# Spreading the mixer's scale rows later, and the rotated key as a task of its own

## The chip, the cores and the metric

The kernel runs on one core of a Trainium2 chip. The metric is the device time of one execution in microseconds (us), as the median over runs. The product stays on TensorE (PE), with weight loads (PEld) beside it; VectorE (DVE) and ScalarE (ACT) prepare operands and empty the accumulators; SyncE (SP) issues the weight transfers.

## What is computed

Two layers of an encoder over 256 tokens of width 2048, all in float32. Each layer is a mixer and a feed-forward block, both on a normalised input and added back. The mixer is cut here to the parts that the change touches:

```python
h = _rms(x, g_mix[l])
proj = h @ w_in
(ml_q, ml_k, ml_v, ml_o, ml_gates, r_q, r_k, r_v, r_g, c_q, c_kv, k_rope) = split(proj)
q = (_rms(c_q, g_q_norm) @ w_q_up)          # 8 heads of 128 + 64, the 64 rotated
kv = (_rms(c_kv, g_kv_norm) @ w_kv_up)      # 8 heads: 128 of key, 128 of value
k_r = _apply_rope(k_rope[:, :, None, :], cos, sin)   # one rotated key, shared by the heads
# mLSTM: gates -> log sigmoid -> cumulative sums; conv of ml_q, ml_k; 4 heads in two directions
# retention of 4 heads; softmax attention of 8 heads; then @ w_out and the feed-forward block
```

## The kernel before

Every product is made of three: each float32 weight is split into a high half `whi` (ACT, L308) and a low half `wlo` (DVE, L309, the raw weight less `whi`), and so are the activations; PE multiplies high by high, high by low and low by high (L410). Weights come as chunks of 512 KB through `Stream` (L230 to L317): four raw buffers, and four buffers each of `whi` and `wlo`. `get(i)` asks for the halves of chunks up to `i + 2`. So a chunk's halves are written into the buffers that PE freed four chunks earlier, and PE has three chunks in hand.

The activations enter as `xT`, the transposed input, not yet normalised. The factor of a token, `rs` (one over the root mean square), is a per-partition scalar where tokens are on partitions; ACT applies it when it empties an accumulator (`ev_cq` L623, `ev_ckv` L649, `ev_rqk` L942). Where tokens lie along the row, it has to be spread over all partitions: `token_scale` (L534) computes `rs` on DVE, has PE transpose it twice into the bank `rsb` (L542) and copies it to SBUF (L543). In a mixer the first reader of that tile is `ev_qk` (L820), after the product for `ml_q`.

Side work is written as generators, `Task`s (L416). After each four to twelve products the program calls `pump` (L453), which advances a clock `now` by the product's nominal time and steps up to two tasks that are free and due: a task is free once the tasks it depends on are done (or have made so many steps), and due once the delay that it last yielded has passed on that clock. `finish` (L441) runs a task to its end on the spot. All this happens while the program is built: what comes out is one fixed order of instructions per engine, and each engine runs its own order strictly.

The weights of a layer's mixer are taken in the order of `weight_plan`. In layer 0: chunks 0 to 8 are `c_q`, 9 to 14 `c_kv` with the rotated part of the key and the gates, 15 to 22 the retention's `r_qk`, 23 and 24 the keys from the latent part (`kn`), 25 and 26 the values (`v`), 27 to 30 the queries (`qn`), 31 and 32 the queries' rotated part (`qr`), and from 33 on `ml_q`, `ml_k`. The tasks around the change are:

- `rope_tables` (L555), once: cosines and sines for the rotation.
- `cq_task` (L626) and `ckv_task` (L654): normalise the latent parts, transpose them (banks `cqt`, `ckvt`) and split them into `chi`, `clo`. `ckv_task` goes on to rotate the key (`rope` into `kr`, ten instructions on DVE, L670 to L672), has PE transpose it twice (`krt`, L676) and splits it into `krh` and `krl`.
- `gate_task` (L742): eight small transposes on PE (`gi`, `gf`), then a chain of small operations that goes between DVE and ACT: exponential and logarithm on ACT, sums, two groups of four scans (L778, L785), maxima and end weights (L791 to L801) on DVE; a row table to HBM (L804), another exponential, and ten small transposes (`gcol`).
- `qr_task` (L681) rotates the queries; `mla_head` needs it and the rotated key.

The product of chunk 23 on reads `chi`, so the program finishes `ckv_task` before it (L1030).

Of the kernel before, what the change touches and what calls it, by code (L numbers as in the profile page):

```python
# [42 lines left out]
G_MIX, G_FFN, G_ML, G_RET, G_Q, G_KV, W_CONV, B_GATE, PAR_W = 0, 16, 32, 36, 40, 44, 46, 70, 86  # L43
# [277 lines left out]
def encoder_kernel(ctx: ExitStack, tc: tile.TileContext, xin, posin, w, par, const, gfin, out, dump=None):  # L321
# [53 lines left out]
    def bank(name):  # L375
        return pside.tile([P, 512], F32, name=name, tag="s")
# [5 lines left out]
    def rsqrt(dst, src, n, scale):  # L382

        nt = sp.tile([P, 3, n], F32, name="nt", tag=f"nt{n}", bufs=2 if n == 2 else 1)
        v, y, a = nt[:, 0, :], nt[:, 1, :], nt[:, 2, :]
        iv = a.bitcast(I32)
        V.tensor_scalar(v, src, scale, EPS, op0=ALU.mult, op1=ALU.add)
        V.tensor_scalar(iv, v.bitcast(I32), 1, None, op0=ALU.arith_shift_right)
        V.tensor_scalar(y.bitcast(I32), iv, -1.0, float(0x5f3759df), op0=ALU.mult, op1=ALU.add)
        for it in range(3):  # L390
            yield 1.0
            V.tensor_tensor(a, y, y, op=ALU.mult)
            V.scalar_tensor_tensor(a, a, -0.5, v, op0=ALU.mult, op1=ALU.mult)
            V.scalar_tensor_tensor(dst if it == 2 else y, a, 1.5, y, op0=ALU.add, op1=ALU.mult)

    def split(*items):

        for hi, lo, src, *g in items:
            A.activation(hi, src, AF.Copy, **({"scale": g[0]} if g else {}))  # L399
        for hi, lo, src, *g in items:  # L400
            if g:
                V.scalar_tensor_tensor(lo, src, g[0], hi.bitcast(F32), op0=ALU.mult, op1=ALU.subtract)
            else:
                V.tensor_tensor(lo, src, hi.bitcast(F32), op=ALU.subtract)

    def tr(dst, src, n=P):
        T.transpose(dst, src, ident[:n, :n])
# [8 lines left out]
    class Task:  # L416
# [24 lines left out]
        def finish(self, n=1 << 30):  # L441
            for d in self.after:
                d, m = d if isinstance(d, tuple) else (d, 1 << 30)
                d.finish(m)
            while not self.done and self.n < n:
                self.step()

    def add(gen, after=(), delay=0.0):
        t = Task(gen, list(after), delay)
        side.append(t)  # L450
        return t
# [33 lines left out]
    def nat(chunks, lh, ll, evac):  # L485
        ps = [pm.tile([P, 512], F32, name="pm", tag="m") for _ in range(2)]
        nat_steps(chunks, ps, lh, ll, 0, True, True)
        evac(ps)
# [16 lines left out]
    xt_task = {}  # L505
# [12 lines left out]
    def make_xT(b, g0, l, wait):  # L518

        xT = views[1 if g0 == G_FFN else 0]  # L520
        for pr in range(2):
            ps = bank("xt")
            for j in range(2):
                k = 4 * b + 2 * pr + j
                for t in range(2):
                    tr(ps[:, j * S + t * P:j * S + (t + 1) * P], x[t][:, k * P:(k + 1) * P])
            k = 4 * b + 2 * pr
            split(*[(xT[:, k + j, 0, :], xT[:, k + j, 1, :], ps[:, j * S:(j + 1) * S],
                     prm[:, l, g0 + k + j:g0 + k + j + 1]) for j in range(2)])
            yield 0.8 if pr == 0 else wait  # L530
        for t in range(2):
            sumsq(x[t][:, b * 512:(b + 1) * 512], ss[:, t, b:b + 1], 512)

    def token_scale():  # L534
        tot = sp.tile([P, 2], F32, name="tot", tag="tot")
        V.tensor_reduce(tot, ss, axis=AX.X, op=ALU.add)
        yield from rsqrt(rs, tot, 2, 1.0 / D)
        yield 1.0
        rsb = sp.tile([P, 2, P], F32, name="rsb", tag="rsb", bufs=1)
        ps = bank("rsb")  # L540
        for t in range(2):
            tr(ps[:, t * P:(t + 1) * P], rs[:, t:t + 1].broadcast_to([P, P]))  # L542
        V.tensor_copy(hflat(rsb), ps[:, :S])  # L543
        scale_rows.append(rsb)

    def new_xT(b, g0, l, wait=0.8):

        xt_task[b] = add(make_xT(b, g0, l, wait), [(xt_task[b - 1], 2)] if b else [])
        if b == 3:
            xt_last[:] = [add(token_scale(), xt_task.values(), 1.2)]  # L550

    xt_last = []
    scale_rows = []
# [55 lines left out]
    def hflat(tl):  # L609
        return tl.rearrange("p a b -> p (a b)")  # L610

    def layer(l):
        g = prm[:, l, :]
        L = {}
# [39 lines left out]
        def ckv_task():  # L654
            ckv = L["ckv"]
            r = sp.tile([P, 2], F32, name="rckv", tag="rckv", bufs=1)
            yield from rsqrt(r, L["sq"][:, 1, :], 2, 1.0 / 256)
            for t in range(2):
                V.tensor_scalar(ckv[:, t, :256], ckv[:, t, :256], r[:, t:t + 1], None, op0=ALU.mult)
            yield 4.0  # L660
            ps = bank("ckvt")
            for k in range(2):
                for t in range(2):
                    tr(ps[:, k * S + t * P:k * S + (t + 1) * P], ckv[:, t, k * P:(k + 1) * P])
            split(*[(L["chi"][:, 4 + k, :], L["clo"][:, 4 + k, :], ps[:, k * S:(k + 1) * S],
                     g[:, G_KV + k:G_KV + k + 1]) for k in range(2)])
            yield 1.0
            kr = ap.tile([P, 2, P], F32, name="kr", tag="kr")
            krh = L["krh"] = ap.tile([P, S], F32R, name="krh", tag="krh")
            for t in range(2):  # L670
                rope(kr[:, t, :64], ckv[:, t, 256:320], t, 1)
                V.tensor_copy(kr[:, t, 64:], kr[:, t, :64])  # L672
            yield 3.0
            ps = bank("krt")
            for t in range(2):
                tr(ps[:, t * P:(t + 1) * P], kr[:, t, :])  # L676
            A.activation(krh, ps[:, :S], AF.Copy)
            V.tensor_tensor(krl[0:64, :], ps[0:64, :S], krh[0:64, :].bitcast(F32), op=ALU.subtract)


        def qr_task():  # L681
            qr = L["qr"]
            qd = ap.tile([P, 2, 8, 2, 64], F32, name="qd", tag="hlo", bufs=2)
            for t in range(2):
                rope(qd[:, t, :, 0, :], qr[:, t, :], t, 8)
                yield 2.4
                A.activation(qd[:, t, :, 1, :], qd[:, t, :, 0, :], AF.Copy)
                yield 1.2

            qrT = L["qrT"] = ap.tile([P, 8, S], F32R, name="qrT", tag="hhi", bufs=2)  # L690
            for pr in range(4):
                ps = bank("qrt")
                for j in range(2):
                    for t in range(2):
                        tr(ps[:, j * S + t * P:j * S + (t + 1) * P],
                           qd[:, t, 2 * pr + j, :, :].rearrange("p i c -> p (i c)"))
                o = hflat(qrT[:, 2 * pr:2 * pr + 2, :])
                A.activation(o, ps, AF.Copy)
                V.tensor_tensor(o[64:128, :], ps[64:128, :], o[64:128, :].bitcast(F32), op=ALU.subtract)
                yield 1.2  # L700
# [114 lines left out]


        def ev_qk(i, pr, ps):
            if "mt" not in L:
                L["mt"] = ap.tile([P, 2, 4, S], F32, name="mt", tag="hlo", bufs=2)
            V.tensor_tensor(L["mt"][:, i, 2 * pr:2 * pr + 2, :], ps.rearrange("p (a b) -> p a b", a=2),  # L820
                            hflat(scale_rows[-1]).unsqueeze(1).broadcast_to([P, 2, S]), op=ALU.mult)
# [202 lines left out]
        nat(take(), xh, xl, ev_cq)  # L1024
        cqt = add(cq_task(), delay=3.0)
        nat(take(), xh, xl, ev_ckv)
        ckt = add(ckv_task(), [(cqt, 1)] + tables, 2.0)
        gat = add(gate_task(), [(ckt, 4)], 1.0)
        nat(take(), xh, xl, ev_rqk)
        finish(ckt)  # L1030
        L["qT"] = ap.tile([P, 8, S], F32, name="qT", tag="big1")
        L["kT"] = ap.tile([P, 8, S], F32, name="kT", tag="big2")
        L["v"] = ap.tile([P, 2, 1024], F32, name="v", tag="big3")
# [19 lines left out]
                A.activation(L["qr"][:, t, :], ps[t], AF.Copy)  # L1053

        nat(take(), chi(0), clo(0), ev_qr)
        qrt = add(qr_task(), [ckt], 2.0)
        heads = []
        for h in range(8):
            dep = [qrt, ckt] if h == 0 else [(heads[-1], 2)] + heads[-2:-1]
            heads.append(add(mla_head(h), dep, 1.2))  # L1060
        rqt = add(rqk_task(), heads[:1], 1.0)
        cv = []
# [14 lines left out]
        for h in range(4):  # L1077
            dep = [cv[1], gat, heads[-1]] if h == 0 else [(mlh[-1], 3)] + [(t, 7) for t in mlh[-2:-1]]
# [32 lines left out]
        for b in range(2):  # L1111
            nat_steps(take(), pss[b], yh, yl, 0, False, True)
            ev_x(b)(pss[b])
            new_xT(b, G_FFN, l)
# [233 lines left out]
    tables = [add(rope_tables(), [xt_task[3]])]  # L1348
    for l in range(DEPTH):
        layer(l)  # L1350
# [29 lines left out]
```

## Time and profile before

| | us |
|---|---|
| median of 3 runs | 2136.35 (2136.01 to 2136.39) |
| the profiled execution, its own time | 2135.27 |
| its span, first to last instruction | 2133.5 |
| PE busy | 2111.1 (99%) |
| DVE busy | 1607.4 (75%) |
| ACT busy | 1218.1 (57%) |
| PE in the chain that ended last | 94% of the span |

The profiled execution stands 1.1 us under the median. The granted clock of TensorE is 0.997 of full speed on the mean. The busy time of PE counts each product until its modelled end, and products overlap in the pipeline, so distances between starts tell more than busy time.

### The profile page before, as it was taken

To read this page: it belongs to the slowest core of one execution; us is meant where nothing else is said; L and a number is where in the kernel's file an instruction comes from. 1 tells how busy PE (TensorE), PEld (TensorE's weight loads), DVE (VectorE), ACT (ScalarE), POOL (GpSimd) and SP (SyncE) were. 2 spreads that over 40 slices of the span, in tenths; PEclk is the share of its full clock that TensorE was granted. 3 is DMA by queue.
4 is the path that set the end of the run, shared out by engine and by line. 5 is a ranking of instruction groups with operands and counts; after the bars stand their busy time and mean duration, and the time that the engine had idled before them with its cause. 6 is when DMAs were issued, how large, how long until landed. Compare 5 with 4: busy or idle time off the path is not lost.

```text
span 2133.5 us, 29557 instructions
## 1 busy us (share of the span) xinstructions
PE 2111.1 (99%) x11120; PEld 1811.4 (85%) x11120; DVE 1607.4 (75%) x2371; ACT 1218.1 (57%) x1802; POOL 4.4 (0%) x9
## 2 busy tenths in 40 slices
PE   8999999999999999999999999999999999999998
PEld 6898888888888888888888988888888888888887
DVE  5667675788878888887666675758888888788875
ACT  6645655556555555565556456546555556565554
POOL 0000000000000000000000000000000000000000
PEclk9999999999999999999999999999999999999999
DMA  6544555647456566565555354557556575665654
GB/s 211 172 155 133 174 168 189 206 163 240 160 209 208 175 210 204 169 237 164 182 181 171 131 172 139 178 188 224 170 206 200 170 236 161 213 211 175 208 187 158
DMA packets 110527, 394.95 MB, mean 185 GB/s; under 512 B 12328, under 2 KB 13224, under 8 KB 110256
## 3 DMA queue, kind: packets, MB, share of 16 engines
q1 hardware_dynamic: 109072, 389.90, 55.8%
q10 hardware_dynamic: 1312, 3.16, 0.4%
q8 instruction: 87, 1.43, 0.3%
q14 instruction: 56, 0.46, 0.1%
HBM read 390.90 MB, written 2.11 MB: 184 GB/s over the span
## 4 chain that ended last, share of the span: by engine, by line
PE 94%; DVE 3%; ACT 1%; DMA 1%; issue 1%; SPq 0%; ACTq 0%; DVEq 0%
PE f L410 33%; PE pm L410 26%; PE pk L410 16%; PE pa L1218 2%; PE pa L1220 2%; PE pa L1219 2%; PE pb L410 2%; PE pd L1218 1%; PE pd L1220 1%; PE pd L1219 1%; DVE wlo L309 1%; PE sc L410 1%; DMA wraw<-in_w_dram 1%; PE pe L1218 1%; PE pe L1220 1%
## 5 line engine op out<-in xcount | busy, mean ns | idle before, releaser
L309 DVE TENSOR_TENSOR wlo<-wraw,whi 128x1024 fp32r<-128x1024 f32 (+2 forms) x681 | 824.9, 1217 | 279.2 <-ACT whi L308 277.3
L308 ACT ACTIVATE whi<-wraw 128x1024 fp32r<-128x1024 f32 (+2 forms) x681 | 704.8, 1050 | 209.8 <-PE f L410 79.5
L410 PE MATMUL f<-xT,whi 128*128 128x512 f32 x2048 | 722.8, 392 | 0.0
L410 PE MATMUL f<-xT,wlo 128*128 128x256 f32 x2048 | 555.7, 282 | 0.0
L410 PEld LDWEIGHTS f<-xT,whi 128*128 128x128 f32 x2048 | 383.5, 188 | 77.5
L410 PEld LDWEIGHTS f<-xT,wlo 128*128 128x128 f32 x2048 | 386.4, 189 | 10.1
L410 PE MATMUL pm<-whi,xT 128*128 128x512 f32 (+1 forms) x896 | 288.7, 391 | 1.4 <-ACT xT L399 1.4
L410 PEld LDWEIGHTS pm<-whi,xT 128*128 128x128 f32 x896 | 167.4, 189 | 31.4 <-ACT xT L399 1.6
L410 PE MATMUL pk<-whi,hhi 128*128 128x512 f32 x496 | 193.7, 391 | 0.0
L410 PE MATMUL pk<-whi,hlo 128*128 128x512 f32 x496 | 193.1, 389 | 0.0
L410 PE MATMUL pk<-wlo,hhi 128*128 128x512 f32 x496 | 192.9, 389 | 0.0
L410 PE MATMUL pm<-wlo,xT 128*128 128x512 f32 (+1 forms) x448 | 171.9, 384 | 2.1 <-DVE wlo L309 2.0
L1135 ACT ACTIVATE fr<-f 128x256 f32<-128x256 f32 x128 | 48.7, 380 | 164.4 <-PE f L410 164.4
L308 ACT ACTIVATE whi<-su 128x1024 fp32r<-128x1024 f32 x84 | 88.7, 1056 | 81.0 <-DVE su L288 68.3
L309 DVE TENSOR_TENSOR wlo<-su,whi 128x1024 fp32r<-128x1024 f32 x84 | 101.4, 1220 | 34.1 <-ACT whi L308 34.1
L410 PEld LDWEIGHTS pk<-whi,hlo 128*128 128x128 f32 x496 | 93.1, 188 | 19.8
L410 PEld LDWEIGHTS pk<-wlo,hhi 128*128 128x128 f32 x496 | 93.1, 188 | 19.4
L410 PEld LDWEIGHTS pk<-whi,hhi 128*128 128x128 f32 x496 | 93.1, 188 | 18.6
L410 PE MATMUL pm<-whi,yhi 128*128 128x512 f32 x256 | 101.5, 397 | 0.0
L410 PEld LDWEIGHTS pm<-wlo,xT 128*128 128x128 f32 x448 | 84.9, 189 | 18.0 <-DVE wlo L309 4.7
L410 PE MATMUL pm<-whi,ylo 128*128 128x512 f32 x256 | 99.9, 390 | 0.0
L410 PE MATMUL pm<-wlo,yhi 128*128 128x512 f32 x256 | 99.6, 389 | 0.0
(295 smaller groups left out, 2979.3 us busy)
## 6 DMA issues: line engine op xcount, KB each, us to landing
wraw<-in_w_dram SPq DMA_DIRECT2D x667, 512.0 KB, 3.9
sb<-in_w_dram SPq DMA_DIRECT2D x56, 512.0 KB, 5.9
wraw<-in_w_dram SPq DMA_DIRECT2D x10, 504.0 KB, 3.4
wt<-mx_rows ACTq DMA_DIRECT2D x8, 256.0 KB, 3.7
out_dram<-xx SPq DMA_DIRECT2D x8, 256.0 KB, 3.1
xx<-in_x_dram SPq DMA_DIRECT2D x3, 512.0 KB, 7.9
gf<-in_gfin_dram ACTq DMA_DIRECT2D x1, 1024.0 KB, 8.4
xx<-in_x_dram SPq DMA_DIRECT2D x2, 256.0 KB, 3.9
```

The source lines that it names most:

```text
L308: self.nc.scalar.activation(hi[:, :f], raw, AF.Copy)
L309: self.nc.vector.tensor_tensor(lo[:, :f], raw, hi[:, :f].bitcast(F32), op=ALU.subtract)
L410: T.matmul(ps, lhsT=lhsT, rhs=rhs, start=start, stop=stop)
L1135: A.activation(r, ps[:, S:], AF.Copy)
L1218: T.matmul(ps, lhsT=ha, rhs=wh, start=st, stop=False, skip_group_check=True)
L1219: T.matmul(ps, lhsT=ha, rhs=wl, start=False, stop=False, skip_group_check=True)
L1220: T.matmul(ps, lhsT=la, rhs=wh, start=False, stop=kp == 3, skip_group_check=True)
```

## The change

`token_scale` yields a lead that its caller gives: 1.0 as before for the feed-forward block, 30.0 for a mixer, so that the transposes of `rs` come when the program's clock has moved on by 30. `ev_qk` finishes the task before it reads the tile. The last third of `ckv_task` becomes `kr_task`, added after the product for `r_qk` and behind `ckv_task` and the tables. `ckv_task` no longer waits for the tables. `gate_task` waits for `kr_task` where it waited for the fourth step of `ckv_task`. `qr_task` and the first head wait for `kr_task`.

```diff
-    def token_scale():
+    def token_scale(lead):
         tot = sp.tile([P, 2], F32, name="tot", tag="tot")
         V.tensor_reduce(tot, ss, axis=AX.X, op=ALU.add)
         yield from rsqrt(rs, tot, 2, 1.0 / D)
-        yield 1.0
+        yield lead
         rsb = sp.tile([P, 2, P], F32, name="rsb", tag="rsb", bufs=1)
...
-            xt_last[:] = [add(token_scale(), xt_task.values(), 1.2)]
+            xt_last[:] = [add(token_scale(1.0 if g0 == G_FFN else 30.0), xt_task.values(), 1.2)]
...
-            yield 1.0
+
+        def kr_task():
+            ckv = L["ckv"]
             kr = ap.tile([P, 2, P], F32, name="kr", tag="kr")
...
         def ev_qk(i, pr, ps):
+            finish(xt_last[-1])
...
-        ckt = add(ckv_task(), [(cqt, 1)] + tables, 2.0)
-        gat = add(gate_task(), [(ckt, 4)], 1.0)
+        ckt = add(ckv_task(), [(cqt, 1)], 2.0)
         nat(take(), xh, xl, ev_rqk)
         finish(ckt)
+        krt = add(kr_task(), [ckt] + tables, 1.0)
+        gat = add(gate_task(), [krt], 1.0)
...
-        qrt = add(qr_task(), [ckt], 2.0)
+        qrt = add(qr_task(), [krt], 2.0)
...
-            dep = [qrt, ckt] if h == 0 else [(heads[-1], 2)] + heads[-2:-1]
+            dep = [qrt, krt] if h == 0 else [(heads[-1], 2)] + heads[-2:-1]
```

No instruction is added or removed on any engine; what the diff moves is seen in the engines' orders. First PE in layer 0, inside the eighth chunk (7) of the product for `c_q`; `pm` are the accumulators, and `rsb` stands for the two transposes of `rs`. Before:

```order
L410 MATMUL pm_132<-whi7_303,xT_80 128x512
L410 MATMUL pm_132<-wlo7_304,xT_80 128x512
L410 MATMUL pm_132<-whi7_303,xT_80 128x512
L407 MATMUL rsb_372<-head_78,rs_83 128x128 x2
L410 MATMUL pm_131<-whi7_303,xT_80 128x512
L410 MATMUL pm_131<-wlo7_304,xT_80 128x512
```

And in the change, where they now stand inside chunk 19, in the product for `r_qk`:

```order
L410 MATMUL pm_581<-wlo19_645,xT_80 128x512
L410 MATMUL pm_581<-whi19_644,xT_80 128x512
L407 MATMUL rsb_701<-head_78,rs_83 128x128 x2
L410 MATMUL pm_580<-whi19_644,xT_80 128x512
L410 MATMUL pm_580<-wlo19_645,xT_80 128x512
```

They moved past eleven chunks; in chunk 7 PE now goes straight on. Second, the two transposes of the rotated key on PE, before between chunks 21 and 22:

```order
L410 MATMUL pm_586<-wlo21_709,xT_80 128x512
L410 MATMUL pm_586<-whi21_708,xT_80 128x512
L407 MATMUL krt_794<-head_78,kr_749 128x128 x2
L410 MATMUL pm_585<-whi22_737,xT_80 128x512
L410 MATMUL pm_585<-wlo22_738,xT_80 128x512
```

And in the change inside chunk 25 (values), with the gates' eight transposes behind that chunk:

```order
L410 MATMUL pm_865<-whi25_782,clo_457 128x512
L407 MATMUL krt_878<-head_78,kr_812 128x128 x2
L410 MATMUL pm_864<-whi25_782,chi_456 128x512
...
L410 MATMUL pm_865<-whi25_782,clo_457 128x512
L407 MATMUL gi_889<-head_78,gt_571 4x128
L407 MATMUL gf_890<-head_78,gt_571 4x128
```

The key's transposes went three and a half chunks down, the gates' from between chunks 18 and 19 to behind chunk 25. Third, DVE in layer 0 around the gates' scans (they read `SCALAR_TENSOR_TENSOR ... x4` here). Before, among the splits of chunks 23 to 26:

```order
L309 TENSOR_TENSOR wlo23_775<-wraw23_653,whi23_774 128x1024
L766 SCALAR_TENSOR_TENSOR g_ab_697<-g_ab_697,g_r_699 4x512
L767 TENSOR_TENSOR g_ab_697<-g_ab_697,g_eu_698 4x512
L678 TENSOR_TENSOR krl_87<-krt_794,krh_750 64x256
L778 SCALAR_TENSOR_TENSOR g_eu_698<-g_ab_697 4x128 x4
L309 TENSOR_TENSOR wlo24_804<-wraw24_679,whi24_803 128x1024
L781 TENSOR_TENSOR g_ab_697<-g_ab_697,g_eu_698 4x512
L785 SCALAR_TENSOR_TENSOR g_eu_698<-g_ab_697 4x128 x4
L309 TENSOR_TENSOR wlo25_835<-wraw25_712,whi25_834 128x1024
```

And in the change, among those of chunks 31 to 33:

```order
L768 SCALAR_TENSOR_TENSOR g_ab_899<-g_ab_899,g_r_901 4x512
L769 TENSOR_TENSOR g_ab_899<-g_ab_899,g_eu_900 4x512
L309 TENSOR_TENSOR wlo31_1001<-wraw31_870,whi31_1000 128x1024
L780 SCALAR_TENSOR_TENSOR g_eu_900<-g_ab_899 4x128 x4
L783 TENSOR_TENSOR g_ab_899<-g_ab_899,g_eu_900 4x512
L309 TENSOR_TENSOR wlo32_1038<-wraw32_912,whi32_1037 128x1024
L787 SCALAR_TENSOR_TENSOR g_eu_900<-g_ab_899 4x128 x4
...
L309 TENSOR_TENSOR wlo33_1080<-wraw33_934,whi33_1079 128x1024
```

The chain moved down by eight chunks; what followed in one go of six to ten small operations behind `wlo25` (L791 to L801) is now cut in two by `wlo33`. Layer 1 moves in the same way.

## Rows read from the trace of the kernel before

**Rows 1.** Page, part 1: busy time, share of the span, instructions.

```profile
PE 2111.1 (99%) x11120; PEld 1811.4 (85%) x11120; DVE 1607.4 (75%) x2371; ACT 1218.1 (57%) x1802; POOL 4.4 (0%) x9
```

**Rows 2.** Waits of PE, whole span: waited for, us in total, times, longest us.

```profile
PE pm L410 <- DVE wlo L309: 5.6, 10, 0.9
PE rsb L407 <- DVE rs L394: 3.2, 1, 3.2
PE krt L407 <- DVE kr L672: 1.9, 4, 0.5
```

**Rows 3.** Timeline of PE, layer 0, around the transposes of `rs`: start, us, what.

```profile
31.35 0.40 PE L410 MATMUL pm<-whi,xT 128*128 128x512 f32 x1
34.91 0.41 PE L407 MATMUL rsb<-head,rs 128*128 128x128 f32 x2 [3.16 <-DVE rs L394]
...
40.66 0.54 PE L410 MATMUL pm<-whi,xT 128*128 128x512 f32 x2
```

**Rows 4.** Windows: stretch, length, busy of PE, PEld, DVE, ACT, POOL, clock, DMA.

```profile
34.90:38.40 3.50, 3.48 (x10) 2.76 (x11) 3.16 (x7) 0.00 (x0) 0.00 (x0) 0.56 0.78 260
66.00:70.00 4.00, 4.00 (x23) 3.19 (x22) 2.50 (x4) 2.02 (x3) 0.00 (x0) 1.00 0.63 213
81.44:95.27 13.83, 12.18 (x74) 10.28 (x73) 13.18 (x28) 10.58 (x16) 0.00 (x0) 1.00 0.48 157
95.27:113.00 17.73, 17.73 (x131) 16.66 (x130) 7.46 (x7) 9.30 (x13) 0.11 (x1) 1.00 0.61 195
1135.41:1149.10 13.69, 12.19 (x74) 10.27 (x72) 13.08 (x28) 10.44 (x16) 0.00 (x0) 1.00 0.49 148
```

**Rows 5.** Timeline of DVE, layer 0: the splits of chunks 8 and 9.

```profile
32.50 1.22 DVE L309 TENSOR_TENSOR wlo<-wraw,whi 128x1024 fp32r<-128x1024 f32 x1
...
34.69 1.21 DVE L309 TENSOR_TENSOR wlo<-wraw,whi 128x1008 fp32r<-128x1008 f32 x1
```

**Rows 6.** Timeline of PE, layer 0: last product before the key's transposes, first behind.

```profile
76.88 0.39 PE L410 MATMUL pm<-whi,xT 128*128 128x512 f32 x1
...
78.61 0.48 PE L410 MATMUL pm<-whi,xT 128*128 128x512 f32 x1
```

**Rows 7.** Chain that ended last: a chunk of 12 and one of 24 products.

```profile
1111.68 2.75 PE pm L410 x12
...
1205.68 2.87 PE pm L410 x24
```

**Rows 8.** Timeline of ACT, layer 0: values emptied, a split, a table, an exponential.

```profile
91.02 1.28 ACT L1043 ACTIVATE v<-pm 128x512 f32<-128x512 f32 x2 [0.78 <-PE pm L410]
...
92.19 1.05 ACT L308 ACTIVATE whi<-wraw 128x1024 fp32r<-128x1024 f32 x1
93.26 1.28 ACT L805 ACT_TABLE_LOAD   x1
94.55 0.63 ACT L805 ACTIVATE g_r<-g_r 4x512 f32<-4x512 f32 x1
```

**Rows 9.** Timeline of DVE, layer 0: the gates' chain between the splits.

```profile
81.58 0.67 DVE L766 SCALAR_TENSOR_TENSOR g_ab<-g_ab,g_r 4x512 f32<-4x512 f32 x1
82.29 0.68 DVE L767 TENSOR_TENSOR g_ab<-g_ab,g_eu 4x512 f32<-4x512 f32 x1
...
83.23 1.35 DVE L778 TENSOR_TENSOR_SCAN g_eu<-g_ab 4x128 f32<-4x128 f32 x4
84.51 1.19 DVE L309 TENSOR_TENSOR wlo<-wraw,whi 128x1024 fp32r<-128x1024 f32 x1
...
86.34 1.36 DVE L785 TENSOR_TENSOR_SCAN g_eu<-g_ab 4x128 f32<-4x128 f32 x4
...
88.74 0.14 DVE L791 TENSOR_TENSOR gsc<-g_eu 4x2 f32<-4x2 f32 x1
...
89.39 0.21 DVE L796 TENSOR_SCALAR g_eu<-g_eu 4x128 f32<-4x128 f32 x1
...
91.35 1.23 DVE L309 TENSOR_TENSOR wlo<-wraw,whi 128x1024 fp32r<-128x1024 f32 x1
```

## The prediction

> **What bounds the kernel.** I read the busy shares first: PE is busy 2111.1 us of a span of 2133.5 [rows 1]. No engine is near it, so the time is PE's products and what interrupts them; a gain has to come out of PE's waits, or out of a slow clock. Second, the list of what PE waited for [rows 2]. Three of its lines belong to the change: one wait of 3.2 us for `rs`, four for the rotated key with 1.9 us together, and ten for low halves with 5.6 us, which are scattered. To see what stands around them I took PE's timeline at the two named waits [rows 3, 6], and windows for the granted clock and for how full the other engines are there [rows 4].
>
> Two things in the windows matter. Behind the wait for `rs` the clock is 0.56 for 3.5 us, the lower of the two levels (1.2 GHz) for most of it; so that wait costs more than its 3.16 us. And from the start of chunk 23 to the start of chunk 27 (keys and values), 13.83 us in layer 0 and 13.69 us in layer 1, DVE is busy 13.18 and 13.08 us: there DVE, not PE, sets the pace. Two chunks of 24 products and two of 12 take 2 x 2.87 + 2 x 2.75 = 11.2 us where nothing interrupts them [rows 7]; so the two stretches lose 2.6 and 2.5 us. In the stretch after it DVE is busy 7.46 of 17.73 us [rows 4]: it has room.
>
> **The transposes of `rs`, layer 0.** Before, the product ahead of them starts at 31.35 us, the next was due 0.23 later (a twelfth of 2.75 [rows 7]) at 31.58, and the first narrow product of `c_kv` starts at 40.66 + 0.23 = 40.89 [rows 3]. Between lie the 6 remaining products of chunk 7 and 12 of chunk 8. In the change PE does the six by 32.95, starts chunk 8 and needs its low half 0.23 later, at 33.2. That split starts at 32.50 and ends at 33.72 on DVE [rows 5]; nothing ahead of it on DVE moves, so PE now waits here, 0.5 us. This is what is late next. Eleven products later it is 36.3; I take 36.4, with a tenth for the restart. Gain: 40.89 - 36.4 = 4.5 us. Behind that nothing new is late: the low half of chunk 9 is there at 34.69 + 1.21 = 35.9 [rows 5], and `rs` itself, which ACT needs to empty `c_q`, is there by 34.9 [rows 3], before the sums end. The two transposes are not saved, only moved into chunk 19: at most their 0.41 us [rows 3]; I charge 0.3. On DVE the copy goes from behind chunk 9's split to chunk 21's, the slot that a longer gate operation leaves. Net 4.2 us. From both sides: 3.16 us less 0.5 and 0.4, if the clock is low anyway, is 2.3; 4.6 if no restart is paid and the transposes hide.
>
> In layer 1 the transposes don't wait: the line for them counts one time [rows 2]. Moving them is worth nothing there.
>
> **The key's transposes.** In layer 0 the last product before them starts at 76.88, the next was due at 77.11 and starts at 78.61 [rows 6]: 1.5 us lost. The waits of layer 1 are the other two of four, of equal size. In the change they stand in the middle of chunk 25, 2.87 + 2.87 + 1.4 = 7.1 us behind the start of chunk 23. The ten DVE operations that make `kr` follow the split of chunk 25, which ACT can feed once it has emptied `r_qk`, about 1.2 us behind that start (the pair of values takes 1.28 [rows 8]); split and rotation take 1.05 + 1.2 + 1.8 more, so `kr` is there at 5.3. Cover 1.8 us; if that cover went, the wait would return, at most the old 1.5. I charge 0.3 for the transposes as above: 1.2 us a layer, 2.4 in all. Bounds: 0 and 3.0.
>
> **The gates' chain.** It leaves the crowded stretch, so the 2.6 and 2.5 us there become free; the question is what it costs in its new place. Count time from the start of chunk 23, without waits. PE: chunk 25 at 5.75; with ten transposes (some 1.2 us, a fifth of it the key's) chunk 26 at 9.7, 27 at 12.4, then 2.87 each: 28 at 15.3, 31 at 23.9, 32 at 26.7, 33 at 29.4, 34 at 32.3. ACT reads the gates' banks at about 9.7 to 10.7 and then has in its queue, ahead of the end of the logarithm: two pairs of values (2.5), three high halves (3.15), two table loads (2.56), exponential and logarithm (1.2), one accumulator (0.6) [rows 8]. Sum 10.0, so the logarithm is there at 20.5, a little less than the sum since these overlap at their ends. From here DVE goes, by the distances of the old order [rows 9]: three operations of 0.6 to 0.7 (1.9), then the low half of chunk 31, 22.4 to 23.6; PE wants it at 23.9 + 0.2. Four scans (1.28) and a subtraction (0.7), low half of 32 at 26.7; wanted at 26.9. Four scans and four small ones (1.28 + 0.65), low half of 33 at 29.8; wanted at 29.65. Six small ones (89.39 to 91.35, 1.96), low half of 34 at 32.9; wanted at 32.7. So the chain just fits: I take 0.4 us of new waits a layer. Net gain 5.1 - 0.8 = 4.3 us. Bounds: 5.1 with no wait left, 0 if all of it comes back.
>
> The rest has one answer. No DMA is moved except the write of the gates' row table, whose readers (the mLSTM heads) come only behind the products for `ml_q`, `ml_k` and `ml_v`; SP's queue keeps its order. POOL is idle. The later `gcol` transposes stand in the middle of chunk 35, 3 us behind the exponential that they need. The rotation of the queries on DVE slips some 2 us against PE, covered by its free time [rows 4].
>
> **Sum.** 4.2 + 2.4 + 4.3 = 10.9 us off the profiled execution's 2135.27 us: 2124.4. The median of the runs shown lies 1.1 us higher, so I forecast 2125.5 us, 0.5% faster.
>
> **A rule against the change.** Eight gate transposes in a row stand in the window from 66 to 70 us and the clock stays at 1.00 [rows 4]; now ten come close together, in a stretch with waits at its end. The Trainium skill, TensorE: Matmul & The Clock Gate, Part 4 (PE-mode transpose), says that transposes don't count as the array being busy in the way that products do; by that rule the clock could fall there, which no row here shows.
>
> **The rivals.**
> - *The chain's waits only move.* My ledger has slacks of 0.2 to 0.5 us; if ACT empties the query accumulators later than I think, every low half from 31 to 34 is late and each layer pays its 2.5 us again. For it: the chain's DVE work comes in lumps of 2 us, and a split of 1.2 behind it fills a chunk of 2.87. Against it: 10 us of free DVE time in the stretch [rows 4]. Gain 10.9 - 4.3 = 6.6: 2129.8 us.
> - *The change does not do what it says for `rs`.* PE then meets DVE's lateness in the next low halves, and the slow clock comes anyway, since PE waited before this too. Against it: the low halves of 8 and 9 end at 33.7 and 35.9 [rows 5]. Gain less 4.2: 2129.7 us.
> - *The clock falls behind the moved transposes*, by the rule above. Worked out from the stretch at 0.56 [rows 4]: 3.5 x 0.44 = 1.5 us a layer, 3.1 in all: 2128.6 us.
> - *The debt reaches the rotated queries.* The gate chain's DVE work is 1.9 + 1.3 + 0.7 + 1.3 + 0.65 + 2.0 and about 1.0 before it, 8.8 us a layer [rows 9]. If it stands whole ahead of the rotation of the queries, the transposes of the rotated queries, inside `ml_q`, wait for it: 8.8 us a layer, and 1.5 more each for the clock, as behind the wait for `rs`. That is 20.6 less 10.9: 2146 us, slower. It decides once DVE is more than 10.9 / 2 = 5.4 us late there. Against it: DVE has 10.3 us free before that point [rows 4], more than the whole chain.
>
> **How the numbers follow.** Forecast 0.67, its own range 2124.0 to 2127.5; chain's waits move 0.17; `rs` without gain 0.07; clock 0.05; debt 0.04. The range reaches over the first two rivals and takes in the bounds: 2123.8 (no new wait, no restart) to 2130.5. Out of it stay the debt and mixtures of rivals. A measurement of this kernel can tell about 0.2%, 4.3 us: below 2132.1 is faster, above 2140.6 slower. All cases but the debt and mixtures lie below 2132.1: faster 0.92, same 0.04, slower 0.04.
>
> **What would show it.** The line of PE's waits for `rs` and the one for `kr` are gone; a wait of about 0.5 us for a low half stands near 33.2 us; the first narrow product starts near 36.4; the clock from 33 to 37 us is 1.0. From chunk 23 to chunk 27 PE takes about 12.4 us, transposes included. Low waits of 0.1 to 0.3 us stand at chunks 33 and 34. Wrong would be: waits of 0.6 to 0.9 us at chunks 31 to 34 (the waits moved), a wait of PE for `qd` (the debt), or a clock under 1 in the stretch of chunk 25.

## The result, and the profile after

| | before | after |
|---|---|---|
| median of the runs, us | 2136.18 (4 runs, 2135.75 to 2136.39) | 2122.66 (4 runs, 2122.50 to 2122.75) |
| profiled execution, us | 2135.27 | 2122.63 |
| its span, us | 2133.5 | 2120.8 |

The ratio is 0.9939, with a 95% interval of 0.9928 to 0.9951: the change takes off 0.6%. The forecast was 2125.5 us with a range from 2123.8 to 2130.5. The direction was right, but the time lies 1.1 us below the range.

The page of the changed kernel, part 1, beside [rows 1]:

```profile
PE 2106.7 (99%) x11120; PEld 1810.5 (85%) x11120; DVE 1607.6 (76%) x2371; ACT 1217.3 (57%) x1802; POOL 4.4 (0%) x9
```

Work is the same on every engine. What changed is what PE waits for: the list of its waits in the changed kernel, to be read against [rows 2] (waited for, us in total, times, longest):

```profile
PE pm L410 <- DVE wlo L309: 3.1, 7, 0.8
PE wps L372 <- DVE warm L369: 1.2, 1, 1.2
PE pm L410 <- ACT xT L399: 1.2, 1, 1.2
```

The lines for `rs` (3.2 us) and for the rotated key (1.9 us) are gone, and of ten waits for low halves (5.6 us) seven are left (3.1 us). PE's timeline of the changed kernel in layer 0 shows the places (start, us, what, the idle time before and its releaser):

```profile
33.71 0.50 PE L410 MATMUL pm<-wlo,xT 128*128 128x512 f32 x1 [0.43 <-DVE wlo L309]
...
36.10 0.54 PE L410 MATMUL pm<-whi,xT 128*128 128x512 f32 x2
36.48 0.32 PE L410 MATMUL pm<-wlo,xT 128*128 128x336 f32 x1
...
64.12 0.39 PE L410 MATMUL pm<-whi,xT 128*128 128x512 f32 x1
64.34 0.38 PE L407 MATMUL rsb<-head,rs 128*128 128x128 f32 x2
64.48 0.48 PE L410 MATMUL pm<-whi,xT 128*128 128x512 f32 x1
...
81.72 0.38 PE L407 MATMUL krt<-head,kr 128*128 128x128 f32 x2
81.86 0.48 PE L410 MATMUL pm<-whi,chi 128*128 128x512 f32 x1
```

The wait for chunk 8's low half, 0.43 us that end at 33.71 and so begin at 33.28, is the one that was forecast for 33.2. Both moved pairs of transposes start without a wait. The windows of the changed kernel, with the columns of [rows 4]:

```profile
33.00:37.00 4.00, 3.57 (x18) 2.84 (x17) 3.79 (x11) 1.12 (x2) 0.00 (x0) 1.00 0.48 143
74.58:86.97 12.39, 12.39 (x83) 11.04 (x82) 5.43 (x14) 8.96 (x15) 0.00 (x0) 1.00 0.48 165
86.97:104.00 17.03, 17.03 (x122) 16.07 (x121) 14.04 (x25) 13.34 (x18) 0.00 (x0) 1.00 0.45 156
1124.41:1136.80 12.39, 12.39 (x83) 11.04 (x82) 5.43 (x14) 8.96 (x15) 0.00 (x0) 1.00 0.52 155
```

The clock is 1.00 from 33 to 37 us, where it was 0.56 behind the transposes of `rs` before. Chunks 23 to 26 take 12.39 us where they took 13.83 and 13.69, and DVE's busy time there fell from 13.2 and 13.1 to 5.4 us. It is now busy 14.0 of 17.0 us in the stretch behind, and PE still has no gap there.

Six marks cut every trace into stretches that can be compared. The marks are the starts of the first narrow product that has a row of its own, of chunk 23 and of chunk 27, in each layer; the rest of a layer lies between its chunk 27 and the next mark, or the end. The very first narrow product is the second of the row above that one and starts 0.15 us earlier (40.89 and not 41.03 in the kernel before, 36.33 and not 36.48 in the changed one); the forecast counts from it. All in us:

| profiled execution of | to the first narrow product | to chunk 23, layers 0 / 1 | to chunk 27, layers 0 / 1 | span |
|---|---|---|---|---|
| before | 41.03 | 40.41 / 40.38 | 13.83 / 13.69 | 2133.5 |
| after | 36.48 | 38.10 / 38.11 | 12.39 / 12.39 | 2120.8 |
| `rows_late_only` | 36.28 | 40.61 / 40.65 | 13.84 / 13.65 | 2128.7 |
| `key_and_gates_only` | 41.62 | 37.89 / 37.86 | 12.39 / 12.39 | 2126.0 |
| `key_apart_gates_early` | 41.21 | 38.78 / 38.77 | 15.57 / 18.29 | 2136.8 |
| `gates_late_key_early` | 40.86 | 38.16 / 38.12 | 12.09 / 12.09 | 2126.2 |
| `rows_and_gates_late` | 36.44 | 38.35 / 38.36 | 12.09 / 12.08 | 2121.8 |

Of the 12.7 us that the span lost, 4.55 lie ahead of the first narrow product, 4.58 in the two stretches to chunk 23, 2.74 in the two behind, 0.43 between chunk 27 of layer 0 and the first narrow product of layer 1 (from 999.76 to 999.33 us) and 0.4 behind chunk 27 of layer 1 (from 984.4 to 984.0).

### The profile page after: what moved, and what is told of

It is laid out like the page before. It is cut to its first block, busy times and chain, and to the rows that moved or that the text cites. A ratio compares the mean times of both kernels' runs of the same rounds, so it can differ in the third digit from the quotient of the medians.

```text
span 2120.8 us, 29557 instructions
## 1 busy us (share of the span) xinstructions
PE 2106.7 (99%) x11120; PEld 1810.5 (85%) x11120; DVE 1607.6 (76%) x2371; ACT 1217.3 (57%) x1802; POOL 4.4 (0%) x9
## 3 DMA queue, kind: packets, MB, share of 16 engines
q10 hardware_dynamic: 1312, 3.16, 0.4%
## 4 chain that ended last, share of the span: by engine, by line
PE 96%; DVE 1%; ACT 1%; DMA 1%; issue 0%; SPq 0%; ACTq 0%; DVEq 0%
PE f L410 34%; PE pm L410 27%; PE pk L410 16%; PE pa L1222 2%; PE pa L1224 2%; PE pa L1223 2%; PE pb L410 2%; PE pd L1222 1%; PE pd L1224 1%; PE pd L1223 1%; PE sc L410 1%; DVE wlo L309 1%; DMA wraw<-in_w_dram 1%; PE pe L1222 1%; PE pe L1224 1%; PE pe L1223 1%
```

## Experiments

**Rows and key apart from each other.** The first two kernels each carry one half of the change. Late scale rows alone:

```diff
-            xt_last[:] = [add(token_scale(), xt_task.values(), 1.2)]
+            xt_last[:] = [add(token_scale(1.0 if g0 == G_FFN else 30.0), xt_task.values(), 1.2)]
...
         def ev_qk(i, pr, ps):
+            finish(xt_last[-1])
```

> Scale rows 30 later, the key and the gates as before. Sum of parts: the 3.16 us wait of TensorE for the token factor goes, and the slow clock behind it; the first narrow product comes at 36.3 us instead of 40.9; nothing else moves. Span 2133.5 - 4.5 = 2129.0 us (2128.5 to 2129.5), waits for the key (1.9 us) and for low halves in the stretch of keys and values stay. If the slow clock were no consequence of that wait, the gain would be 2.3 to 3.0 and the span 2130.5 to 2131. If the parts were not independent (the earlier arrival runs into a later wait), the gain is partly lost behind and the span is 2131 to 2133.

Measured: 2130.52 us (9 runs), ratio 0.9976, 0.9966 to 0.9985. The wait for `rs` and the low clock went (1.00 from 34.90 to 38.40), the key's four waits stayed (1.9 us), and one low-half wait came (eleven, 6.2 us). The span fell by 4.8 us, a little more than the 4.2 that the prediction credited.

The whole change, but with the rows spread where they were:

```diff
-            xt_last[:] = [add(token_scale(1.0 if g0 == G_FFN else 30.0), xt_task.values(), 1.2)]
+            xt_last[:] = [add(token_scale(1.0), xt_task.values(), 1.2)]
```

> Scale rows as before, key apart and gates behind it. Sum of parts: the wait of 3.2 us for the token factor stays with its slow clock; from chunk 22 on it runs as in the whole change. Span 2133.5 - (12.7 - 4.5) = 2125.3 us (2124.8 to 2126), 4.1 us less per layer. If the whole change's gain in layer 0 needed both parts, the span is above 2127.

Measured: 2127.49 us (4 runs), ratio 0.9960, 0.9945 to 0.9975. The profiled execution is this kernel's slowest, with a span of 2126.0. From the first narrow product to chunk 27 it gains 3.96 us in layer 0 and 3.82 in layer 1; ahead of them it loses 0.59, since the clock stayed low longer behind the wait for `rs` in this profile (0.63 from the transposes to the first narrow product, 6.93 us; 0.72 and 6.12 us in the kernel before). So the two halves add up to the whole: 4.8 and 7.5 us of span are 12.3 against 12.7, and the 0.59 us lost ahead more than make up the difference.

**The key's own task without the gates' move.** The changed kernel with early rows, and the gates' chain back ahead of `r_qk`:

```diff
         ckt = add(ckv_task(), [(cqt, 1)], 2.0)
+        gat = add(gate_task(), [(ckt, 4)], 1.0)
...
-        gat = add(gate_task(), [krt], 1.0)
```

> Only the key's rotation and its two transposes move; the gates' chain stays among the splits of chunks 23 to 26, the scale rows early. Sum of parts: the key's waits go (1.3 us per layer), the low halves of the stretch are still late, by about 2 us per layer, less what the key's 1.8 us of VectorE work made of it. Span 2130 to 2131 us. Rival, the key's work and not the gates' crowds VectorE: then the low halves are in time here and the span is 2126 or less.

Measured: 2137.53 us (10 runs), ratio 1.0009, 1.0000 to 1.0019; span 2136.8, 3.3 us over the kernel before and 5.8 over the expected range. The profile is of this kernel's slowest execution (2138.57); by the medians on this chip it is 2.0 us slower than the kernel before (2135.54). The expected gain is not there either way. PE's timeline of this kernel:

```profile
90.44 0.33 PE L407 MATMUL krt<-head,kr 128*128 128x128 f32 x1 [1.85 <-DVE kr L674]
91.26 0.33 PE L407 MATMUL krt<-head,kr 128*128 128x128 f32 x1 [0.50 <-DVE kr L674]
```

And DVE's, from the small operations that end the gates' chain to the last of the ten that make `kr`:

```profile
87.01 0.14 DVE L793 TENSOR_TENSOR gsc<-g_eu 4x2 f32<-4x2 f32 x1
...
89.14 0.41 DVE L803 TENSOR_SCALAR g_eu<-g_eu 4x512 f32<-4x512 f32 x1
89.48 0.21 DVE L602 TENSOR_TENSOR rp<-ckv,cosf 128x64 f32<-128x64 f32 x1
...
91.01 0.20 DVE L674 COPY kr<-kr 128x64 f32<-128x64 f32 x1
```

The key leaves the stretch ahead of chunk 23, which becomes 1.6 us shorter, but it now stands on DVE behind the end of the gates' chain, and PE waits 2.35 us for it in layer 0 and 2.22 in layer 1, where it had waited 0.96 and 0.95. The later place is only free if the chain is gone from there. That the key's own move ends its waits, on which the forecast's 2.4 us rested, fell here.

**The gates' move without the key's.** The kernel before, with the gates added behind the latent task:

```diff
-        gat = add(gate_task(), [(ckt, 4)], 1.0)
         nat(take(), xh, xl, ev_rqk)
         finish(ckt)
+        gat = add(gate_task(), [ckt], 1.0)
```

> Only the gates' chain moves behind the latent part's end; the key stays in its old place, the scale rows early. Sum of parts: the waits for the key stay (1.9 us, four times), the late low halves of chunks 23 to 26 go, and no new ones come: 2.5 us per layer, span 2128 to 2129 us. Rival, the key's work crowds VectorE: the low halves stay late and the span is 2131 to 2133.

Measured: 2127.86 us (5 runs), ratio 0.9963, 0.9949 to 0.9977. The profiled span is 2126.2. The late low halves of chunks 24 and 26 are gone, as expected. In the kernel before, PE's timeline has them here:

```profile
85.76 0.38 PE L410 MATMUL pm<-chi,wlo 128*128 128x256 f32 x1 [0.91 <-DVE wlo L309]
...
92.63 0.50 PE L410 MATMUL pm<-wlo,chi 128*128 128x512 f32 x1 [0.75 <-DVE wlo L309]
```

In one point the expectation missed, and the span is 1.8 us under its range: the key's transposes still stand ahead of chunk 23, but their waits, which were to stay, are gone. The reason is a step earlier, on ACT. In the kernel before, ACT's timeline has two table loads and an exponential of the gates around chunk 22's high half:

```profile
72.69 1.28 ACT L758 ACT_TABLE_LOAD   x1
73.98 0.63 ACT L758 ACTIVATE g_eu<-g_eu 4x512 f32<-4x512 f32 x1
74.52 1.04 ACT L308 ACTIVATE whi<-wraw 128x1024 fp32r<-128x1024 f32 x1
75.58 1.28 ACT L763 ACT_TABLE_LOAD   x1
```

DVE then stands idle 2.02 us for that high half, and the rotation is queued behind its low half; DVE's timeline of the kernel before:

```profile
75.59 1.23 DVE L309 TENSOR_TENSOR wlo<-wraw,whi 128x1024 fp32r<-128x1024 f32 x1 [2.02 <-ACT whi L308]
76.74 0.22 DVE L602 TENSOR_TENSOR rp<-ckv,cosf 128x64 f32<-128x64 f32 x1
```

In the kernel with late gates and early key, DVE does the same three microseconds sooner, and `kr` (ready at 75.45) is there when PE comes at 76.03. First DVE, then PE:

```profile
72.56 1.23 DVE L309 TENSOR_TENSOR wlo<-wraw,whi 128x1024 fp32r<-128x1024 f32 x1
73.71 0.22 DVE L602 TENSOR_TENSOR rp<-ckv,cosf 128x64 f32<-128x64 f32 x1
...
75.25 0.20 DVE L672 COPY kr<-kr 128x64 f32<-128x64 f32 x1
```

```profile
76.03 0.38 PE L407 MATMUL krt<-head,kr 128*128 128x128 f32 x2
```

Of the three microseconds 1.9 are the table load and the exponential that no longer stand ahead of the high half. The rest is that ACT's split of the latent part comes sooner (70.74 in place of 71.83), mostly because PE no longer has the gates' eight transposes ahead of it. So the gates' chain made both the late low halves of chunks 24 and 26 and the key's waits.

A kernel with late rows and late gates, but with the key left in the latent task, tells what the key's own task is worth:

```diff
-            xt_last[:] = [add(token_scale(), xt_task.values(), 1.2)]
+            xt_last[:] = [add(token_scale(1.0 if g0 == G_FFN else 30.0), xt_task.values(), 1.2)]
...
-        gat = add(gate_task(), [(ckt, 4)], 1.0)
...
         finish(ckt)
+        gat = add(gate_task(), [ckt], 1.0)
```

> The kernel before with the scale rows late (lead 30 and the finish in the decay product's eviction) and the gates' chain added behind the latent part, but the rotated key left inside the latent task: the whole change without the key's own task. Theory (rows and gates are all of the gain, and the key's split costs or gives under 1 us): 2122.0 to 2123.5 us, with no wait for `kr` and none for `rs`, 0.4 to 1.0 us over the changed kernel through low halves that come late at the rotated query's chunks. Rival (the key's task is what gives the 2.4 us that were forecast for it, in the presence of the late rows): 2124.5 to 2125.5 us and waits for `kr` of about 0.5 us in each of four pairs.

Measured: 2123.61 us (4 runs, 2123.46 to 2123.86), span 2121.8: 1.0 us over the changed kernel, with no wait for `rs` or `kr`. The theory holds, if 0.1 us above its range: the key's task is worth 1.0 us by the profiled executions. Without it the gates' chain starts a step earlier. The stretch to chunk 27 becomes 0.3 us shorter and the one ahead 0.25 longer, but the 118.1 us from chunk 27 to PE's next listed wait for a low half (at 213.37 before, at 205.09 in the changed kernel) become 118.7 in each layer. The late low halves that were expected at the rotated queries' chunks make up most of that, though the list of PE's waits, still at seven low halves and 3.0 us, does not count them. PE at chunk 31:

```profile
98.39 0.39 PE L410 MATMUL pm<-whi,chi 128*128 128x512 f32 x1
98.80 0.50 PE L410 MATMUL pm<-wlo,chi 128*128 128x512 f32 x1
99.14 0.39 PE L410 MATMUL pm<-whi,clo 128*128 128x512 f32 x1
```

DVE ends that chunk's low half at 98.75. The starts lie 0.41 and 0.34 us apart, and 0.34 and 0.33 at chunk 32 (101.43, 101.77, 102.10), where 0.23 is usual: 0.5 us in all. Such a delay is too short to be listed, since the product ahead counts as busy for 0.39 us.

**How far the rows have to move.** The changed kernel with another lead:

```diff
-token_scale(1.0 if g0 == G_FFN else 30.0)
+token_scale(1.0 if g0 == G_FFN else 4.0)
```

> The changed kernel with a lead of 4 in place of 30 in the mixer, which puts the scale rows' transposes of layer 0 behind chunk 8, some 5 us later than in the kernel before instead of 33. Theory (all that matters is that `rs` is there when TensorE comes to them): `rs` is ready at 34.9, the transposes start near 36.5 without a wait, 2122.3 to 2123.0 us as the changed kernel. Rival (the far move is needed, since transposes among the early chunks cost a restart and a slower clock, or the evictions of the rows on VectorE make another low half late): a wait of 0.3 us or more for `rs` or `wlo` near 36 to 39, 2123.5 to 2125 us.

Measured: 2122.28 us (4 runs, 2122.17 to 2122.71), span 2120.9 in the slowest of the four: as the changed kernel. PE's timeline of this kernel has the pair behind chunk 8, without a wait:

```profile
36.39 0.38 PE L407 MATMUL rsb<-head,rs 128*128 128x128 f32 x2
36.52 0.40 PE L410 MATMUL pm<-whi,xT 128*128 128x336 f32 x1
```

Some 1.5 us later than 34.9 would do; the rest of the 33 us in lead is not needed.

**The clock behind the wait.** The kernel before, with 13 spare products ahead of the transposes in layer 0:

```diff
+        wps = bank("wps") if warm else None
+        for _ in range(warm):
+            mm(wps, views[0][:, 0, 0, :P], hflat(views[0][:, 0, :, :]))
         ps = bank("rsb")
```

> The kernel before with one addition: 13 spare products of the first input block with itself (128x512 outputs into a bank of their own, never read) ahead of the scale rows' transposes in layer 0, so that TensorE multiplies in the 3.16 us in which it waited for `rs` in the profile of before. At the 0.23 us from start to start of such products they last 3.0 us, so the transposes start where they did, at 34.9 to 35.2. Theory (the wait costs twice: its own 3.2 us, and a granted clock of 0.56 behind it): the clock stays at 1.00, the seventeen products from the transposes to the first narrow one take some 4.3 us in place of 6.1, so that one starts at 39.3 to 39.7 in place of 41.03; 2134.0 us, between 2133.6 and 2134.4, and the executions stand closer together than the kernel before's. Rival (the stretch behind the transposes is slow for another reason, such as evictions that come late): first narrow product at 41.0 or later, 2135.3 to 2136.5.

Measured: 2133.35 us (10 runs, 2133.15 to 2133.93), ratio 0.9992, 0.9983 to 1.0001, against a kernel before of 2134.98 on that chip (13 runs, 2134.52 to 2136.01). PE's timeline of this kernel:

```profile
31.62 3.11 PE L410 MATMUL wps<-xT 128*128 128x512 f32 x13
34.95 0.40 PE L407 MATMUL rsb<-head,rs 128*128 128x128 f32 x2 [0.22 <-DVE rs L394]
...
39.47 0.32 PE L410 MATMUL pm<-wlo,xT 128*128 128x336 f32 x1
```

A window of it, with the columns of [rows 4]:

```profile
34.95:38.40 3.45, 3.44 (x16) 2.88 (x17) 3.16 (x7) 0.00 (x0) 0.00 (x0) 1.00 0.73 260
```

The transposes start where they did, but from them to the first narrow product it takes 4.52 us in place of 6.12 (34.91 to 41.03), and the clock in the window is 1.00, where it was 0.56 in the kernel before. So the 4.55 us that the late rows gave in layer 0 are made up of 3.16 for the wait, 1.6 for the clock behind it and some 0.2 for the pair that left, less the 0.43 us that PE waits at 33.71 instead: 4.5 us. The median is 0.25 us under the theory's range; the kernel before was also lower on that chip, by 0.29 us against its first profiled execution. The interval of the ratio reaches one, but on that chip the executions of the two kernels do not overlap.

**The kernel before once more**, unchanged:

> The kernel before, unchanged, in other executions and with another profile. Theory (its executions differ by how long the clock stays low behind the 3.16 us wait for `rs`, and by little else): in the new profile the stretch from the transposes of `rs` to the first narrow product is between 5.9 and 7.0 us (6.12 in the profile of before), and the profiled execution's time less that stretch is 2129.15 us within 0.15, as in the profile of before (2135.27 - 6.12); the executions spread over 1 us or more. Rival (they differ elsewhere, in transfers or in the feed-forward part): the time less that stretch moves by 0.3 us or more.

Measured: 2135.53 us (11 runs, 2132.82 to 2136.27). The new profile's stretch is 6.10 us and its time less that stretch 2129.12, within what was expected; but since the stretch is almost that of the first profile, this alone does not show that executions differ by it. It speaks for it that the stretch was 6.93 us in the profile of `key_and_gates_only`, that kernel's slowest execution, and that the spread shrank to 0.8 us with the spare products (10 runs), 0.6 with the late rows alone (9) and 0.25 in the changed kernel (4). The mean clocks on record go the same way, though coarsely: of the 58 executions of the kernel before on the three chips of the experiments, the 14 listed at 0.998 have a median of 2134.7 us and the 11 at 0.996 one of 2135.6. The two profiles of this kernel lie only 0.05 us apart and the execution at 2132.82 has none, so what the executions differ by is not shown.

**A version that is faster than both.** Three of the seven low-half waits that are left stand in the chunks 6 to 8 of layer 0. ACT's timeline of the changed kernel shows four sums of squares between two high halves:

```profile
20.20 1.09 ACT L308 ACTIVATE whi<-wraw 128x1024 fp32r<-128x1024 f32 x1
...
24.07 1.04 ACT L308 ACTIVATE whi<-wraw 128x1024 fp32r<-128x1024 f32 x1
...
27.89 3.86 ACT L308 ACTIVATE whi<-wraw 128x1024 fp32r<-128x1024 f32 x4
```

A chunk of 12 products takes 2.75 us [rows 7], and with four sums a high half comes every 3.85 us. The edit makes the blocks' sums due one after the other:

```diff
     for b in range(4):
-        new_xT(b, G_MIX, 0, 5.0)
+        new_xT(b, G_MIX, 0, (3.0, 4.5, 6.0, 6.0)[b])
```

> The changed kernel with one more edit: in layer 0 the four blocks' sums of squares no longer become due together (all with a wait of 5.0) but at 3.0, 4.5, 6.0 and 6.0, so that ScalarE has fewer of them between two high halves of the c_q chunks 6, 7 and 8. Theory (the three low-half waits of 0.43, 0.76 and 0.43 us at these chunks, with restarts some 1.9 us in all, come from ScalarE making the high halves late behind four sums in a row): they fall to 0.5 us together, the first narrow product starts at 34.9 to 35.6 in place of 36.48, 2121.0 to 2121.8 us. Rival (the sums only move, and the late half with them, or `rs` becomes late for the c_q evictions): 2122.4 us or more, with waits of the same size at other chunks.

Measured: 2120.93 us (4 runs, 2120.83 to 2121.02), ratio to the kernel before 0.9934, 0.9919 to 0.9949. On the same chip the lead of 4, which is as fast as the changed kernel, took 2122.28, and the executions of the two do not overlap. Median and start come out just under what was expected (2121.0 and 34.9). PE's waits in this kernel:

```profile
PE pm L410 <- ACT xT L399: 2.3, 1, 2.3
PE pm L410 <- DVE wlo L309: 1.4, 4, 0.5
```

All three waits are gone, where I had expected 0.5 us of them to stay, and the first narrow product starts at 34.76 in place of 36.48, although the first chunk's weights were there 0.8 us later here. On ACT, high halves now start at 21.41, 23.73, 26.05 and 28.37, with two sums between.

## Why the prediction was wrong in size

Two terms of the sum above all put the time below the range: the 1.1 us that I added to the profiled execution, and the 0.8 us of new waits behind the moved gates' chain, of which none came. A third was right in its number by luck: the key's waits went for another reason than the one I gave.

**The transposes of `rs`, layer 0.** Right in mechanism and close in size: first narrow product forecast at 36.4, measured, counted the same way, 36.10 + 0.23 = 36.33; wait of 0.5 from 33.2 on forecast, 0.43 from 33.28 on measured; gain 4.5 forecast, 4.55 measured. I charged 0.3 us for the transposes in their new place; the two products around them start 0.36 apart (64.12 to 64.48) in place of 0.23, the next one 0.31 behind (64.79), and so the pair costs some 0.2.

**Layer 1.** The prediction put the move at nothing, since the pair did not wait. It did cost PE something in its old place: `rows_late_only` gains 0.45 us between the layers and loses 0.27 in the next stretch, 0.2 net.

**The key's transposes.** The 2.4 us came, but by luck: for another reason than I gave. I credited them to the key's own move. `key_apart_gates_early` shows that this move alone only carries the waits along, and `gates_late_key_early` that they end without it. I had looked at who PE waits for (DVE, `kr`) and not at what DVE waits for one step before (2.02 us for ACT's high half, behind the gates' table load and exponential). The key's own part is 1.0 us in both layers together.

**The gates' chain.** The stretch to chunk 27 is 12.39 us, as forecast (12.4). The step that failed is the 0.4 us of new waits that I took a layer: none came, at chunks 33 and 34 or elsewhere, and the 118.1 us behind chunk 27 are the same before and after to 0.02. DVE's timeline of the changed kernel:

```profile
94.50 0.68 DVE L766 SCALAR_TENSOR_TENSOR g_eu<-g_eu 4x512 f32<-4x512 f32 x1 [0.71 <-ACT g_r L765]
...
96.43 1.21 DVE L309 TENSOR_TENSOR wlo<-wraw,whi 128x1024 fp32r<-128x1024 f32 x1
...
99.56 1.21 DVE L309 TENSOR_TENSOR wlo<-wraw,whi 128x1024 fp32r<-128x1024 f32 x1
...
102.73 1.21 DVE L309 TENSOR_TENSOR wlo<-wraw,whi 128x1024 fp32r<-128x1024 f32 x1
```

Counted from chunk 23 at 74.58, my ledger had the logarithm at 20.5 and the low halves of chunks 31 to 33 ending at 23.6, 26.7 and 29.8. They end at 23.1, 26.2 and 29.4, since the logarithm is there by 19.9: ACT goes through the queue that I summed to 10.0 us in 9.2 (85.26 to 94.47 on its timeline), since its entries overlap at their ends. I had named these overlaps and taken off 0.2 us for them; they are worth 0.8. With slacks of 0.2 us the sign of a wait hung on that.

**The end.** Every kernel here with the gates early takes 19.5 to 19.6 us from the next-to-last wait of PE for a low half to the end of the span, every one with the gates late 19.2. It comes from one gap on DVE in the final normalisation. In the kernel before:

```profile
2124.92 0.15 DVE L1323 TENSOR_REDUCE sqf<-ss 128x1 f32<-128x3 f32 x1
2125.54 0.16 DVE L1324 TENSOR_TENSOR sqf<-sqf 128x1 f32<-128x1 f32 x1 [0.47 <-DVE sqf L1323]
```

and in the changed kernel:

```profile
2112.63 0.15 DVE L1327 TENSOR_REDUCE sqf<-ss 128x1 f32<-128x3 f32 x1
2112.88 0.16 DVE L1328 TENSOR_TENSOR sqf<-sqf 128x1 f32<-128x1 f32 x1
```

Program and operands are the same there. Why the gap closes stays open; no view that I read of the kernel before could have shown that it would.

**The base.** I added 1.1 us, by which the profiled execution of before stood under its median. The changed kernel has no such distance (2122.63 profiled, 2122.66 median). If the distance comes from the clock behind the wait for `rs`, as the spreads suggest, the change takes it away with the wait, and it should have been counted as a gain and not carried over. No run shows its cause; what the runs show is that with the rows late and nothing else changed (`rows_late_only`) the profiled execution stands at the median, 2130.52.

Together: of the 2.8 us between forecast and result, 1.1 are the base, 0.8 the new waits that did not come, 0.4 the end, 0.2 layer 1 and some 0.3 the transposes that cost 0.2 and not 0.3 a pair. The low end of the range, 2123.8, carried the same base, and so missed: its bounds of 4.6, 3.0 and 5.1 us add up to 12.7, and the two profiled executions differ by 12.64.

**The rivals** did not come: no wait at chunks 31 to 34, no wait for `rs`, no wait for `qd`. The clock is 1.00 in the stretch with ten transposes, 74.58 to 86.97: two of them start at 81.72 and eight in a row from 83.33 to 84.09, with products ahead and behind, and PE has no gap. The rule that spoke against the change is that of the Trainium skill, TensorE: Matmul & The Clock Gate, Part 4 (PE-mode transpose), by which transposes do not count as the array being busy in the way that products do; it cost nothing here.

## What to carry to other kernels

When an engine waits for a small result, follow the producer's own queue back one more engine before crediting the move of that result: here a table load and an exponential on ScalarE were most of the cause, and moving the waiting step alone moved the wait with it. A wait of TensorE costs more than its length where the clock falls behind it (here 3.16 us and 1.6 more). The kernels with such a wait also scattered more between executions here; why is not shown, but a forecast for a change that removes the wait should carry both bases, the profiled execution and the median, into its range. Where a ledger's slack is smaller than the overlaps it leaves out, take both signs into the range.

## What the runs showed that I had not expected

Two equal waits do not always have the same price. In `key_apart_gates_early` PE waits 1.85 and 0.50 us for the key in layer 0, and 1.87 and 0.35 us in layer 1. The windows of the two stretches from chunk 23 to chunk 27, and of five microseconds in the second:

```profile
79.99:95.56 15.57, 12.53 (x75) 10.48 (x74) 14.44 (x38) 9.62 (x14) 0.00 (x0) 1.00 0.43 148
1134.07:1152.36 18.29, 15.38 (x76) 12.51 (x74) 14.70 (x38) 11.01 (x16) 0.00 (x0) 0.81 0.43 147
1144.00:1149.00 5.00, 4.13 (x10) 3.10 (x11) 3.79 (x11) 1.56 (x4) 0.00 (x0) 0.54 0.27 77
```

In layer 0 the clock stayed at 1.00; in layer 1 it was at 0.54 over five microseconds, the lower level of 1.2 GHz for most of them, and the stretch took 2.7 us more. This profile is of the slowest of ten executions, so how often that happens is not shown. Behind the wait of 3.16 us for `rs` the clock fell in each of the five profiles that have that wait (0.50 to 0.65 from 34.90 to 38.40). The start of the fall moves too: in the kernel before a product at the slower pace stands right behind the transposes (35.43, 0.63 us), and in its second profile the first such one starts at 36.08.
